# Rotary embedding on half the head: tiles of 64 KB runs, three resident, one product in PSUM, last tile in halves

## The chip, the cores and the metric

One NeuronCore of a Trainium2 chip. Times are device microseconds of the core for one execution; "span" is the time from the first to the last instruction in a profiled execution, about 2 us shorter (160.4 us of 162.49 in the kernel before). Each kernel ran in turns with the kernel before on the same chip. The experiments ran in later jobs, on several chips and not in the changed kernel's rounds, so they are compared with it through the kernel before. An execution over 1.5% above the fastest of the same kernel is classed slow.

## The reference, cut to what matters

```python
x: (16, 512, 16, 64) float32          # batch, seq, heads, dim
x1, x2 = x[..., :32], x[..., 32:]
first  = x1[..., :16] * cos[..., :16] - x1[..., 16:] * sin[..., :16]
second = x1[..., :16] * sin[..., :16] + x1[..., 16:] * cos[..., :16]
out = concatenate([first, second, x2], axis=-1)
```

33.55 MB are read and 33.55 MB written. Half of every row (x2) is only copied. On the other half there are four multiplications and two additions for each pair of elements.

## The kernel before

A tile holds K = 8 sequence positions on each of 128 partitions, a contiguous run of 32 KB a partition, 4 MB in all. There are eight tiles and five buffers. Loads are issued from SP, stores from ACT; both queues draw on the same 16 DMA engines (in the profile before, 49.3% and 48.7% of the time of 16; loads alone, up to 32 us, moved 403 and 437 GB/s, loads and stores together 431 to 433).

```python
K = 8
x_pool = tile_pool(name="xp", bufs=5)
ab_pool = tile_pool(name="abp", bufs=1)
... # cos and sin loaded from ACT, spread to all partitions by 4 VectorE copies
KC = 4
for t in range(T):                                   # T = 8
    x_t = x_pool.tile([P, K, H, D], fp32)
    nc.sync.dma_start(out=x_t..., in_=xf[t])
    for k0 in range(0, K, KC):
        x1 = x_t[:, k0 : k0 + KC, :, 0:HF]
        ...
        nc.vector.tensor_mul(out=a_t[:], in0=x1, in1=c)
        nc.vector.tensor_mul(out=b_t[:], in0=x1, in1=s)
        nc.vector.tensor_sub(out=x1[..., 0:Q],  in0=a_t[..., 0:Q],  in1=b_t[..., Q:HF])
        nc.vector.tensor_add(out=x1[..., Q:HF], in0=a_t[..., Q:HF], in1=b_t[..., 0:Q])
    nc.scalar.dma_start(out=of[t], in_=x_t...)
```

## Time and profile before

| | before |
|---|---|
| time, median | 162.49 us (3 runs) |
| span of the profiled run | 160.4 us |
| both data queues' share of 16 DMA engines | 98.0% |
| VectorE busy | 110.8 us (69%) |
| last tile's data in, last store issued | 128.3 us, 142.1 us |

The lines that carry this stand in the prediction. In the timeline: start, duration, engine, line, operation, output and inputs, count, and in brackets the idle time before it with what ended it.

### The profile page before, as it was taken

To read this page: it belongs to the slowest core of one execution; us is meant where nothing else is said; L and a number is where in the kernel's file an instruction comes from. 1 tells how busy PE (TensorE), PEld (TensorE's weight loads), DVE (VectorE), ACT (ScalarE), POOL (GpSimd) and SP (SyncE) were. 2 spreads that over 40 slices of the span, in tenths; PEclk is the share of its full clock that TensorE was granted. 3 is DMA by queue.
4 is the path that set the end of the run, shared out by engine and by line. 5 is a ranking of instruction groups with operands and counts; after the bars stand their busy time and mean duration, and the time that the engine had idled before them with its cause. 6 is when DMAs were issued, how large, how long until landed. Compare 5 with 4: busy or idle time off the path is not lost.

```text
span 160.4 us, 155 instructions
## 1 busy us (share of the span) xinstructions
DVE 110.8 (69%) x68; POOL 0.2 (0%) x4
## 2 busy tenths in 40 slices
DVE  0001599999999999999998799609995099940000
POOL 0000000000000000000000000000000000000000
DMA  7999999999999999999999999999999999999993
GB/s 253 408 400 408 392 417 490 400 408 498 400 400 474 433 392 457 457 392 449 466 392 417 490 400 408 498 400 400 476 425 400 466 441 400 449 457 400 417 482 147
DMA packets 2465, 67.25 MB, mean 419 GB/s; under 512 B 288, under 2 KB 416, under 8 KB 416
## 3 DMA queue, kind: packets, MB, share of 16 engines
q1 hardware_dynamic: 1152, 33.55, 49.3%
q10 hardware_dynamic: 1312, 33.69, 48.7%
q14 instruction: 1, 0.01, 0.0%
HBM read 33.69 MB, written 33.55 MB: 419 GB/s over the span
## 4 chain that ended last, share of the span: by engine, by line
DMA 53%; DVE 30%; issue 4%; DVEq 1%; ACTq 0%; SPq 0%
DMA x_t<-in_x_dram 21%; DMA out_dram<-x_t 21%; DVE b_t L66 11%; DMA stage<-in_sin_dram 10%; DVE a_t L65 10%; DVE x_t L70 5%; DVE x_t L67 4%; DVEq L99 1%; ACTq L41 0%; DVE table L48 0%; SPq L58 0%; DVEq L65 0%
## 5 line engine op out<-in xcount | busy, mean ns | idle before, releaser
L65 DVE TENSOR_TENSOR a_t<-x_t,table 128x2048 f32<-128x2048 f32 x16 | 36.7, 2292 | 13.6 <-DMA x_t<-in_x_dram 13.2
L66 DVE TENSOR_TENSOR b_t<-x_t,table 128x2048 f32<-128x2048 f32 x16 | 36.5, 2284 | 0.0
L67 DVE TENSOR_TENSOR x_t<-a_t,b_t 128x1024 f32<-128x1024 f32 x16 | 19.6, 1226 | 0.6
L70 DVE TENSOR_TENSOR x_t<-a_t,b_t 128x1024 f32<-128x1024 f32 x16 | 19.5, 1218 | 0.0
L48 DVE COPY table<-stage 64x256 f32<-64x256 f32 x4 | 1.1, 287 | 17.1 <-DMA stage<-in_cos_dram 12.2
L88 POOL MEMSET const-bfloat16-1.0<- 128x1 bf16 x1 | 0.1, 102 | 0.0
L88 POOL MEMSET const-uint8-127<- 128x1 uint8 x1 | 0.1, 102 | 0.0
L88 POOL MEMSET const-float32-0.0<- 128x1 f32 x1 | 0.1, 99 | 0.2 <-issue 0.2
L88 POOL MEMSET const-float32-1.0<- 128x1 f32 x1 | 0.1, 99 | 0.0
## 6 DMA issues: line engine op xcount, KB each, us to landing
x_t<-in_x_dram SPq DMA_DIRECT2D x8, 4096.0 KB, 33.9
out_dram<-x_t ACTq DMA_DIRECT2D x8, 4096.0 KB, 31.3
stage<-in_cos_dram ACTq DMA_DIRECT2D x1, 64.0 KB, 11.4
stage<-in_sin_dram ACTq DMA_DIRECT2D x1, 64.0 KB, 16.3
```

What stands on the lines that cost most here:

```text
L48: nc.vector.tensor_copy(out=table[r * PB : (r + 1) * PB, t], in_=stage[:, t, :, 0:Q].unsqueeze(2).to_broadcast((PB, K, 2, Q)),)
L65: nc.vector.tensor_mul(out=a_t[:], in0=x1, in1=c)
L66: nc.vector.tensor_mul(out=b_t[:], in0=x1, in1=s)
L67: nc.vector.tensor_sub(out=x1[:, :, :, 0:Q], in0=a_t[:, :, :, 0:Q], in1=b_t[:, :, :, Q:HF])
L70: nc.vector.tensor_add(out=x1[:, :, :, Q:HF], in0=a_t[:, :, :, Q:HF], in1=b_t[:, :, :, 0:Q])
L88: nc = _bacc.Bacc("TRN2", target_bir_lowering=False, num_devices=1)
L99: with _tile.TileContext(nc) as tc:
```

## The change

The intent: longer runs per DMA packet and fewer, longer VectorE operations. A tile of K = 16 has runs of 64 KB; three of them are resident. To make room (the author's reckoning), one product goes to PSUM and the other is formed in place. Only the last tile is cut in halves, so that its first half can be computed and stored early. GpSimd takes half of the table copies.

```diff
-    K = 8
+    K = 16
-    x_pool = ctx.enter_context(tc.tile_pool(name="xp", bufs=5))
-    ab_pool = ctx.enter_context(tc.tile_pool(name="abp", bufs=1))
+    x_pool = ctx.enter_context(tc.tile_pool(name="xp", bufs=3))
+    b_pool = ctx.enter_context(tc.tile_pool(name="bp", bufs=1, space=bass.MemoryType.PSUM))
...
+        eng = nc.vector if r % 2 == 0 else nc.gpsimd      # table copies, cos and sin in one
...
-    KC = 4
+    KC = 8
+    loads = [[16]] * (T - 1) + [[8, 8]]
+    stores = [[16]] * (T - 1) + [[8, 8]]
...
-            nc.vector.tensor_mul(out=a_t[:], in0=x1, in1=c)
             nc.vector.tensor_mul(out=b_t[:], in0=x1, in1=s)
+            nc.vector.tensor_mul(out=x1, in0=x1, in1=c)
...              # sub and add now read x1 and b_t; a piece is stored when its last rows are done
```

More of the change, by code (lines that the diff above doesn't have):

```diff
@@ L29 @@
     REP = P // PB
+    R = H * D
     xf = x.rearrange("b s h d -> (b s h d)").rearrange("(t p f) -> t p f", t=T, p=P)
@@ L46 @@
     for r in range(REP):
-        for t in range(2):
-            nc.vector.tensor_copy(
-                out=table[r * PB : (r + 1) * PB, t],
-                in_=stage[:, t, :, 0:Q].unsqueeze(2).to_broadcast((PB, K, 2, Q)),
-            )
+        eng = nc.vector if r % 2 == 0 else nc.gpsimd
+        eng.tensor_copy(
+            out=table[r * PB : (r + 1) * PB].rearrange("p t k c j -> p (t k) c j"),
+            in_=stage.rearrange("p t k j -> p (t k) j")[:, :, 0:Q]
+            .unsqueeze(2)
+            .to_broadcast((PB, 2 * K, 2, Q)),
+        )
     C = table[:, 0].rearrange("p k c j -> p k (c j)")
     Sn = table[:, 1].rearrange("p k c j -> p k (c j)")
-    KC = 4
+    KC = 8
+    loads = [[16]] * (T - 1) + [[8, 8]]
+    stores = [[16]] * (T - 1) + [[8, 8]]
     for t in range(T):
         x_t = x_pool.tile([P, K, H, D], fp32)
-        nc.sync.dma_start(out=x_t.rearrange("p k h d -> p (k h d)"), in_=xf[t])
+        x_f = x_t.rearrange("p k h d -> p (k h d)")
+        k0 = 0
+        for n in loads[t]:
+            nc.sync.dma_start(
+                out=x_f[:, k0 * R : (k0 + n) * R], in_=xf[t, :, k0 * R : (k0 + n) * R]
+            )
+            k0 += n
+        ends, k0 = [], 0
+        for n in stores[t]:
+            ends.append((k0, k0 + n))
+            k0 += n
         for k0 in range(0, K, KC):
@@ L62 @@
             s = Sn[:, k0 : k0 + KC].unsqueeze(2).to_broadcast((P, KC, H, HF))
-            a_t = ab_pool.tile([P, KC, H, HF], fp32)
-            b_t = ab_pool.tile([P, KC, H, HF], fp32)
-            nc.vector.tensor_mul(out=a_t[:], in0=x1, in1=c)
+            b_t = b_pool.tile([P, KC, H, HF], fp32)
             nc.vector.tensor_mul(out=b_t[:], in0=x1, in1=s)
+            nc.vector.tensor_mul(out=x1, in0=x1, in1=c)
             nc.vector.tensor_sub(
-                out=x1[:, :, :, 0:Q], in0=a_t[:, :, :, 0:Q], in1=b_t[:, :, :, Q:HF]
+                out=x1[:, :, :, 0:Q], in0=x1[:, :, :, 0:Q], in1=b_t[:, :, :, Q:HF]
             )
             nc.vector.tensor_add(
-                out=x1[:, :, :, Q:HF], in0=a_t[:, :, :, Q:HF], in1=b_t[:, :, :, 0:Q]
+                out=x1[:, :, :, Q:HF], in0=x1[:, :, :, Q:HF], in1=b_t[:, :, :, 0:Q]
             )
-        nc.scalar.dma_start(out=of[t], in_=x_t.rearrange("p k h d -> p (k h d)"))
+            for lo, hi in ends:
+                if hi == k0 + KC:
+                    nc.scalar.dma_start(
+                        out=of[t, :, lo * R : hi * R], in_=x_f[:, lo * R : hi * R]
+                    )
 _INS = ['x', 'cos', 'sin']
```

## The prediction

> **What bounds the kernel now.** I read the two-line summary of queues first, because the kernel does almost no arithmetic per byte: 33.55 MB in, 33.55 MB out.
>
> ```profile
> DVE 110.8 (69%) x68; POOL 0.2 (0%) x4
> DMA  7999999999999999999999999999999999999993
> ...
> q1 hardware_dynamic: 1152, 33.55, 49.3%
> q10 hardware_dynamic: 1312, 33.69, 48.7%
> ```
>
> The queues' shares are of the time of 16 DMA engines: 49.3 + 48.7 = 98.0%. Only 2.0% of 160.4 us, 3.2 us per DMA engine, is not spent on a packet. VectorE is busy for 69%. The slices show where the 3.2 us lie: 7 in the first slice and 3 in the last, 9 (90% or more) everywhere else. Then the windows, cut where the work changes (columns: stretch, its length, VectorE busy, POOL busy, clock, DMA share, GB/s):
>
> ```profile
> 4.00:20.00 16.00, 2.86 (x5) 0.00 (x0) 1.00 0.98 403
> 20.00:32.00 12.00, 11.90 (x8) 0.00 (x0) 1.00 1.02 437
> 32.00:60.00 28.00, 27.69 (x18) 0.00 (x0) 1.00 1.00 431
> 60.00:100.00 40.00, 37.94 (x22) 0.00 (x0) 1.00 1.00 433
> 100.00:128.00 28.00, 16.72 (x11) 0.00 (x0) 1.00 1.00 431
> ```
>
> Loads alone (to 32 us) and loads with stores (after it) run at the same rate, about 432 GB/s at a share of 1.00: the DMA engines are full, whichever direction. A packet is booked where it ends, so short windows wobble. The rest is the start and the compute times:
>
> ```profile
> 0.73 0.54 ACTq L41 DMA_DIRECT2D stage<-in_cos_dram  x1
> 0.73 93.59 SPq L58 DMA_DIRECT2D x_t<-in_x_dram  x8
> 1.30 0.61 ACTq L42 DMA_DIRECT2D stage<-in_sin_dram  x1
> ...
> 17.67 0.59 DVE L48 COPY table<-stage 64x256 f32<-64x256 f32 x2 [4.90 <-DMA stage<-in_sin_dram]
> 18.29 2.29 DVE L65 TENSOR_TENSOR a_t<-x_t,table 128x2048 f32<-128x2048 f32 x1
> ```
>
> VectorE starts only at 18.29 us because two 64 KB table loads land at 12.2 and 17.7 us, behind the x loads. That lateness is free: the DMA engines are busy with five tiles of loads meanwhile. VectorE later idles three times for a load (13.2 us in the waits), which is also free: it waits for the full DMA engines. The chain of waits puts 53% on DMA and 30% on DVE, but that chain follows the buffers; the DVE part of it (18 to 60 us) lies under full DMA engines.
>
> From the packet records of the trace: a 32 KB packet takes 1213 ns, a 1 KB packet 46 ns, the first data packet starts at 1.7 us and the last completion is at 159.2 us. Each engine has 128 packets of 32 KB: 128 x 1.213 = 155.3 us. With 1.7 us in front and 1.2 us behind that makes 158.2 of the 160.4; some 2 us are gaps and small packets, most before 23 us. The median of 162.49 us is 2.1 us above the span.
>
> [...]the 64 KB cosine load needs 11.4 us to land, its packets taking turns with 32 KB packets of x.[...]
>
> **The change part by part.**
>
> Bytes: the same 67.1 MB. That alone fixes about 155 us.
>
> Runs of 64 KB in place of 32 KB: 46 ns for 1 KB and 1213 ns for 32 KB give (1213 - 46)/31 = 37.6 ns per KB and a fixed part of 46 - 37.6 = 8.4 ns a packet. A 64 KB run should take 2 x 1213 - 8.4 = 2418 ns. Of the 128 packets per engine, the 96 of the first three quarters become 48; the last tile keeps 32 KB. So 48 x 8.4 ns = 0.4 us saved. The DMAs drop from 18 to 12, six completions of 9 ns. So **-0.45 us**, on the path.
>
> VectorE: 64 operations become 32. Half a tile costs [...]2 x 4.42 us and 2 x 2.29 us, 13.4 us, where two quarters of today cost 2 x 6.92 (18.29 to 25.21). Over 8 halves 107 us for 110.7[...]. All beside DMA: **0 us**. What counts is only whether VectorE's times still feed the DMA queues with tiles of 8 MB, four of them, three resident.
>
> Tables: each load is now 32 rows of 2 KB, so 2 packets and a completion per engine in place of 4 and one; but each turn is a 64 KB packet of 2.42 us. Today the first cosine packet starts at 5.9 us, about 3.5 packets of x after 1.7. I take 3 to 3.5 turns of 2.42: 9.5 to 10.2 us. Six turns later (3 for each table) both tables are in at about 22 to 24 us; tile 0, 8 x 2.42 us, lands at about 22 too. Then two copies on VectorE[...] and two on POOL at the side[...]. VectorE starts at about s = 25 to 27 us, not 18.3. Take 26.
>
> The schedule from there, in us, with 19.4 for 8 MB when alone:
> - Loads 0 to 2 (24 MB) keep DMA busy until about 61 (1.7 + 24 x 2.42 + 1.3 of start gaps).
> - Tile 0 is done at 26 + 26.7 = 53 and its store is issued. Today the first store, issued at 32.14, moves data at 36.0, 3.2 packets later; now 3.2 x 2.42 = 7.7, so at about 60: still before the loads run out. Store 0 ends at 61 + 19.4 = 80.5.
> - Tile 1 is done at 53 + 26.7 = 79.4: store 1 is queued just as store 0 ends. The load of tile 3 needs the buffer of tile 0, is issued at 80.5 plus some 0.5 us to signal, and moves data 1 us after that (as today's first load: issued 0.73, moving 1.73). **This is the one thin seam**: store 1 fills it if s is 26, else there is a gap of up to 1.5 to 2 us. I book **+0.5 us**.
> - From 80.5 store 1 and load 3 take turns: both done at about 119.5. Tile 2 is done at 106, so store 2 is queued behind store 1. Half 3a landed at about 100 and is done at 119.5; half 3b lands at 120 and is done at 133.5. Stores 2, 3a, 3b are then 16 MB from 119.5 on: 158.5. Both halves are queued long before their turn, so loading and storing the last tile in halves adds and saves nothing.
>
> Sum: 162.5 - 0.45 + 0.5, less some 0.3 us for fewer small packets at the start (my guess): **162.2 us**.
>
> **The rivals.**
> 1. *The seam opens.* If tables and tile 0 are later (s = 32 or more), store 0 comes after the loads run out at 61 and store 1 some 5 us after store 0 ends. For it: eight-megabyte steps, only three buffers. Against: load 3 fills the second hole after 2 us. It would make 164 to 166.
> 2. *VectorE becomes the bound.* For it: PSUM operands and in-place multiplies are new. Against: it may end its last half as late as about 146 (158 - 9.7 for a 4 MB store, and some margin) against 133.5 expected; 12 us over 107 is 11% slower operations. In that case up to 164.
> 3. *Long runs are better than the line says, or start and tail shrink.* [...]A gain of 2% (3.25 us) would need more than all the time in which DMA is idle now, and the 2.9 us of first and last latency in that are not touched.
> 4. *Long runs are worse* (64 KB cut into pieces[...]). Nothing in the trace speaks for it; 1% of rate is 1.6 us.
>
> **Range and chances.** The byte count fixes 155 us and nothing but gaps can add. [...]likely 161.5 to 162.8, a seam of 2 us 164. Range 161.0 to 164.0. Faster by over 2% needs what rival 3 excludes: 0.02. Slower by over 2% (165.7) needs rival 1 in full or two rivals at once: 0.04. Within 2%: 0.94.
>
> **What the profile after would show.** Queue shares again near 98% in sum, with 1280 data packets of x and not 2048 (if 2048, the runs were cut). VectorE near 108 us busy, 4.42 and 2.29 us operations, first multiply at 25 to 27 us. DMA slices of 9 throughout; a dip only near 60 or 80 us. Last multiply done at about 133. The prediction is wrong if a slice in the middle falls under 9, [...]or if the last store is issued after 146 us.

The sum came to 162.2 us, from 162.5 - 0.45 + 0.5 and less some 0.3. Its 0.3 was a guess at a part of the 2 us of gaps and small packets in the profile before, and is not shown. The profile before alone leads to the same 4.42 us by an estimate: 1226 ns for 1024 elements and 2292 for 2048 are 1066 for 1024 more, so 2292 + 2 x 1066 = 4424 for 4096.

## More of the kernel before

```profile
128.30 2.29 DVE L65 TENSOR_TENSOR a_t<-x_t,table 128x2048 f32<-128x2048 f32 x1 [5.90 <-DMA x_t<-in_x_dram]
...
135.22 2.29 DVE L65 TENSOR_TENSOR a_t<-x_t,table 128x2048 f32<-128x2048 f32 x1
...
140.89 1.22 DVE L70 TENSOR_TENSOR x_t<-a_t,b_t 128x1024 f32<-128x1024 f32 x1
```

The reader is to see that 14 us of VectorE work follow the last load's landing. They cost nothing, because the DMA engines are still full (share 1.04, 447 GB/s, from 128 to 142 us): earlier stores wait in the queue.

## The result, and the profile after

| | before | changed |
|---|---|---|
| median, same rounds | 162.45 us (6 runs) | 171.87 us (6 runs, 170.94 to 174.04) |
| ratio of the fast runs | | 1.056 (95%: 1.0531 to 1.0588) |

A ratio is the mean time of one kernel's fast runs over that of the other's fast runs in the same rounds, so it is not quite the ratio of the medians. The change is 5.6% slower; 162.2 us within 161.0 to 164.0 had been predicted.

The execution profiled with these times was a slow one (173.62 us). The changed kernel was therefore run again unedited, twice. The first of those runs is a single execution with a profile at 174.27 us; its state is unknown, its time that of slow ones. The second, on the chip of a later job, gave 168.23 and 168.54 us as fast and 172.98 and 173.74 as slow executions, with a profile of a fast one (span 166.8 us). Against the mean of the kernel before in that job, 162.5 us, its two fast executions are 3.6% slower (two executions, so without an interval), not 5.6%: how large the loss is differs between jobs. That fast profile, busy tenths in 40 slices and queues' shares:

```profile
DVE 108.9 (65%) x34; POOL 3.2 (2%) x6
DVE  0000439999999999999999999008993001999000
DMA  7979979996997999799698889999888989950885
q1 hardware_dynamic: 720, 33.55, 47.4%
q10 hardware_dynamic: 816, 33.69, 46.7%
```

The shares sum to 94.1%, not 98.0%. Single sevens and sixes in the DMA row are the booking of long packets where they end (around the second 6, from 70 to 95 us, at least 15 packets are in flight in the packet records); the 5 and the 0 late in the row are a real hole. The windows around it (stretch, its length, VectorE busy, POOL busy, clock, DMA share, GB/s):

```profile
108.00:141.00 33.00, 13.34 (x4) 0.00 (x0) 1.00 0.99 429
141.00:149.00 8.00, 7.86 (x2) 0.00 (x0) 1.00 0.91 393
149.00:155.00 6.00, 5.49 (x3) 0.00 (x0) 1.00 0.00 0
155.00:165.00 10.00, 0.00 (x0) 0.00 (x0) 1.00 0.98 419
```

From 149 to 155 us nothing is moved while VectorE computes; then the last 4 MB are stored alone. The timeline says why VectorE is so late:

```profile
81.90 1.03 SPq L68 DMA_DIRECT2D x_t<-in_x_dram  x2
...
113.32 4.43 DVE L81 TENSOR_TENSOR b_t<-x_t,table 128x4096 f32<-128x4096 f32 x1 [9.01 <-DMA x_t<-in_x_dram]
...
126.76 28.13 ACTq L91 DMA_DIRECT2D out_dram<-x_t  x2
141.11 4.43 DVE L81 TENSOR_TENSOR b_t<-x_t,table 128x4096 f32<-128x4096 f32 x1 [14.38 <-DMA x_t<-in_x_dram]
...
152.24 2.28 DVE L86 TENSOR_TENSOR x_t<-x_t,b_t 128x2048 f32<-128x2048 f32 x1
```

The last tile's two loads are issued at 82 us. The first half is used from 113.3 us and the second from 141.1 us. The prediction had 100 and 120. The last store is issued at 154.6 us.

The groups of the VectorE (line, engine, operation, output and inputs, shape, count | busy us, mean ns of one | idle us before, and what ended most of it) show that its operations cost what was predicted:

```profile
L81 DVE TENSOR_TENSOR b_t<-x_t,table 128x4096 f32<-128x4096 f32 x8 | 35.5, 4433 | 26.3 <-DMA x_t<-in_x_dram 26.1
L82 DVE TENSOR_TENSOR x_t<-x_t,table 128x4096 f32<-128x4096 f32 x8 | 35.4, 4425 | 0.3
L83 DVE TENSOR_TENSOR x_t<-x_t,b_t 128x2048 f32<-128x2048 f32 x8 | 18.3, 2288 | 0.3
L86 DVE TENSOR_TENSOR x_t<-x_t,b_t 128x2048 f32<-128x2048 f32 x8 | 18.2, 2280 | 0.0
L50 DVE COPY table<-stage 32x1024 f32<-32x1024 f32 x2 | 2.1, 1056 | 18.8 <-DMA stage<-in_sin_dram 18.8
L50 POOL COPY table<-stage 32x1024 f32<-32x1024 f32 x2 | 2.9, 1474 | 18.4 <-DMA stage<-in_sin_dram 18.4
```

The slow execution with which the median was reported has the same hole, only wider; its slices:

```profile
DVE  0000449999999999999999993008992000999100
DMA  7989995999889996999799989999989999700885
```

There the second half is used from 146.2 us and the last store is issued at 159.6 us. In the packet records the DMA engines are without work for 10.6 us on average before that store, against 6.6 us in the fast profile. The spans exceed that of before by 11.4 and 6.4 us: in these two profiles the hole is the loss, to within 1 us.

### The profile page after: what moved, and what is told of

It reads as the page before. It is cut to its first block, busy times and chain, and to the rows that moved or that the text cites. A ratio compares the mean times of both kernels' runs of the same rounds, so it can differ in the third digit from the quotient of the medians.

```text
span 171.8 us, 108 instructions
## 1 busy us (share of the span) xinstructions
DVE 108.8 (63%) x34; POOL 3.1 (2%) x6
## 4 chain that ended last, share of the span: by engine, by line
DVE 45%; DMA 33%; another core or an unknown queue 9%; issue 3%; DVEq 1%
DMA x_t<-in_x_dram 33%; DVE b_t L81 18%; DVE x_t L82 15%; DVE x_t L86 7%; DVE x_t L83 5%; DVEq L119 1%; DVEq L81 0%
## 5 line engine op out<-in xcount | busy, mean ns | idle before, releaser
L81 DVE TENSOR_TENSOR b_t<-x_t,table 128x4096 f32<-128x4096 f32 x8 | 35.5, 4432 | 31.1 <-DMA x_t<-in_x_dram 30.9
L82 DVE TENSOR_TENSOR x_t<-x_t,table 128x4096 f32<-128x4096 f32 x8 | 35.4, 4424 | 0.3
L83 DVE TENSOR_TENSOR x_t<-x_t,b_t 128x2048 f32<-128x2048 f32 x8 | 18.3, 2286 | 0.3
L86 DVE TENSOR_TENSOR x_t<-x_t,b_t 128x2048 f32<-128x2048 f32 x8 | 18.2, 2280 | 0.0
L50 DVE COPY table<-stage 32x1024 f32<-32x1024 f32 x2 | 2.1, 1056 | 19.1 <-DMA stage<-in_sin_dram 19.1
L50 POOL COPY table<-stage 32x1024 f32<-32x1024 f32 x2 | 2.9, 1474 | 18.8 <-DMA stage<-in_sin_dram 18.7
```

Source lines behind the costliest of these rows:

```text
L50: eng.tensor_copy(out=table[r * PB : (r + 1) * PB].rearrange("p t k c j -> p (t k) c j"), in_=stage.rearrange("p t k j -> p (t k) j")[:, : ...
L82: nc.vector.tensor_mul(out=x1, in0=x1, in1=c)
L83: nc.vector.tensor_sub(out=x1[:, :, :, 0:Q], in0=x1[:, :, :, 0:Q], in1=b_t[:, :, :, Q:HF])
L86: nc.vector.tensor_add(out=x1[:, :, :, Q:HF], in0=x1[:, :, :, Q:HF], in1=b_t[:, :, :, 0:Q])
```

## The experiments

**The theories.** P: the DMA engines take turns between the load queue and the store queue packet by packet. A packet here is a run (in the records of each data queue 384 packets of 64 KB and 256 of 32 KB, in the slow profile), so the last tile's 32 KB load packets beside 64 KB store packets get a third of the rate, not a half. The data comes late, the stores that should cover its computation are used up, and a hole opens. B: with three resident tiles the last load is issued too late, at 82 us, whatever its packets. V: half-tile VectorE operations, 13.4 us before a store can start, are too long at the end, or are slowed by PSUM. "Idle" in what follows is the time for which, by the packet records, fewer than 14 of the 16 DMA engines have a packet, in the middle of the run, as a mean over the engines.

### The last tile loaded whole

```diff
-    loads = [[16]] * (T - 1) + [[8, 8]]
+    loads = [[16]] * T
```

> The last tile is loaded by one DMA in 64 KB runs, everything else as in the changed kernel. Theory P (the DMA engines take turns packet by packet between loads and stores, so a 32 KB load packet beside a 64 KB store packet gets a third of the rate): with equal packets the load gets half, 8 turns of 4.84 us from about 86 us, so the last tile's data is in at about 125 us and not at 146; both its halves are computed by 152, the DMA engines stop for some 3 us instead of 10.6, time about 165 to 166 us. Rival B (three resident tiles: the load is issued too late, at 82 us, whatever its packets): the data is still in at about 146, and now no half of the tile can start before, so the time rises by a half tile's 13.4 us to about 184 us.

Measured: 166.58 us median of 4 (163.65 to 167.3); only the fastest was classed fast, so there is no ratio with an interval. In the profile (a slow one at 166.29 us):

```profile
125.56 4.43 DVE L81 TENSOR_TENSOR b_t<-x_t,table 128x4096 f32<-128x4096 f32 x1 [21.55 <-DMA x_t<-in_x_dram]
...
139.00 4.43 DVE L81 TENSOR_TENSOR b_t<-x_t,table 128x4096 f32<-128x4096 f32 x1
...
150.13 2.28 DVE L86 TENSOR_TENSOR x_t<-x_t,b_t 128x2048 f32<-128x2048 f32 x1
```

With twice the packet, the whole 8 MB are in at 125.6 us, earlier than the second half of it had been, though the load is issued at the same 82.2 us. Idle 3.7 us before the last store, and 0.6 us at 139 us, where the next to last store was issued just as the one before it ended. P had said 125, 152 and some 3 us. The time that it gave, 165 to 166 us, none of the four runs met: the fast one is below it, the slow ones are above. B had said 146, and falls as a sole cause. This is the cleanest of the experiments: only the load differs, one DMA in 64 KB runs in place of two in 32 KB runs.

### Stores in 32 KB runs

```diff
+                    cut = 8 if t < T - 1 else 8
+                    for p0 in range(lo, hi, cut):      # two DMAs in place of one
-                    nc.scalar.dma_start(out=of[t, :, lo*R : hi*R], in_=x_f[:, lo*R : hi*R])
+                        nc.scalar.dma_start(out=of[t, :, p0*R : (p0+cut)*R], in_=x_f[:, p0*R : (p0+cut)*R])
```

> The first three tiles are still loaded in 64 KB runs, computed and stored at the same moments, but each store is two DMAs of half a tile, so that stores move in 32 KB packets like the last tile's two loads. Theory P: the loads get half the rate, first half in at about 103 us, second at about 122, last operation at about 135, no stretch without DMA in the middle, time 161.5 to 163.5 us. Rival B (late issue with three buffers): second half in at about 146 as in the changed kernel, time about 171. Rival V (half-tile VectorE operations are too long at the end): the tail after the last load is the same 13.4 us of operations and a 4 MB store, time about 171.

Measured: 162.04 us median of 4, ratio 0.998 (0.9942 to 1.0017): the loss is gone. The slices show no hole:

```profile
DVE  0000239999999999999999999939990599700000
DMA  7969699699699999999999999999999999999991
```

The first half is used from 107.4 us, the second from 126.8, and the last store is issued at 140.2. P had said 103, 122 and 135: the order is right, the moments are some 4 to 5 us later, for the load moved its first data only at 86.8 us. One thing was not as I had written: the framework let the first of the two stores go as soon as its half was done (the first store of all at 37.4 us, not 50.9), so packets were not all that changed. The last load was issued no earlier for it, at 83.0 us. V falls as a sole cause: the half-tile operations are all still there.

### The mix turned round

```diff
-    loads = [[16]] * (T - 1) + [[8, 8]]
+    loads = [[16]] * T                 # with the 32 KB stores of the experiment above
```

> The mix turned round: last tile loaded whole in 64 KB runs, stores of the first three tiles in 32 KB runs. Theory P: the load gets two thirds of the rate, 8 turns of 3.63 us from about 86 us, so all of the last tile is in at about 115 to 116 us; it is computed at about 142, before the earlier stores have drained, time 161.5 to 163.5 us. Rival B: in at about 146 us, time about 184.

Measured: 162.11 us median of 4, ratio 0.997 (0.9947 to 0.9997).

```profile
81.94 0.33 SPq L68 DMA_DIRECT2D x_t<-in_x_dram  x1
...
114.64 4.43 DVE L81 TENSOR_TENSOR b_t<-x_t,table 128x4096 f32<-128x4096 f32 x1 [10.07 <-DMA x_t<-in_x_dram]
```

Issued at the same moment as in the changed kernel, all 8 MB are in at 114.6 us, where the changed kernel has half of them. P had said 115 to 116.

### The last half in quarters

```diff
-        for k0 in range(0, K, KC):
+        for k0, KC in ((0, 8), (8, 8)) if t < T - 1 else ((0, 8), (8, 4), (12, 4)):
-    stores = [[16]] * (T - 1) + [[8, 8]]
+    stores = [[16]] * (T - 1) + [[8, 4, 4]]
```

> Packets of the loads as in the changed kernel (32 KB loads beside 64 KB stores), but the last half tile is computed and stored as two quarters. Theory P: the second half is still in only at about 146 us; the first quarter is stored from 154 us on while the second is computed until 160, so the last store is 2 MB in place of 4 MB, 4.85 us shorter: about 166.5 us, still over 2% slower than before. If the half-tile operations alone were the cause (rival V), the time would come back to about 162.5.

Measured: 168.62 us median of 4 (167.28 to 169.79), ratio 1.035 (1.0268 to 1.0440). The second half was used from 144.6 us; the hole is cut in two, 3.4 and 2.1 us. The time is some 2 us above what I wrote. Shorter operations at the end don't remove the loss. Whether they soften it is not shown: the ratio is below the 1.056 of the changed kernel's first job, and about the 3.6% of its later one.

### A smaller load packet still

```diff
-    loads = [[16]] * (T - 1) + [[8, 8]]
+    loads = [[16]] * (T - 1) + [[4, 4, 4, 4]]
```

> The last tile's load cut into four DMAs of 16 KB runs; stores stay at 64 KB. Theory P: the load now gets a fifth of the rate as long as stores are queued, so its first half (16 packets of 16 KB per engine, each beside a 64 KB store packet, turns of 3.03 us from about 86 us) is in only at about 134 us and not at 116; the stores then run out and the second half follows alone, in at about 144 to 145 us. Both halves are computed after that, last operation at about 161, time about 174 to 175 us. If the share did not depend on the packet's size, the first half would stay at about 116 us and the time at 171.

Measured: 171.2 us median of 4 (168.46 to 175.16), ratio 1.043 (1.0363 to 1.0498). My numbers missed: the first half was used from 127.7 us (not 134, though not 116 either), the second from 143.0, and the two fast runs took 168.46 and 170.29 us, not 174. The share itself was as P says (table below). What I had left out is that stores with four fifths of the rate (79%, table below) use up their own queue: store 1 was through at about 105 us, the next was issued at 104.8 and moved its first data 3.4 us later, and in between the load had the engines nearly alone (308 GB/s from 104 to 110 us in the packet records). The changed kernel has a smaller patch of the same kind (in its slow profile the load has 99 to 100% of the bytes from 108 to 110 us, at 381 to 389 GB/s), which is most likely why its second half is in at 140.6 us and not at 86 + 16 x 3.63 = 144.

The share of the load in all bytes moved while both queues were full, from the packet records:

| | load / store packets | share by packet sizes | measured, 86 to 104 us |
|---|---|---|---|
| last tile's load in 16 KB | 16 / 64 KB | 20% | 21% |
| changed kernel, fast profile | 32 / 64 KB | 33% | 33% |
| load whole | 64 / 64 KB | 50% | 53% |
| stores in 32 KB | 32 / 32 KB | 50% | 53% |
| mix turned round | 64 / 32 KB | 67% | 73% |

In 18 us there are only 4 to 7 turns, so some points of difference are to be expected.

In all these runs a piece is one DMA, so a smaller packet is also a smaller DMA, and the edits don't tell which of the two sets the share. The packet records do. In the fast profile 155 packets of x start from 86 to 104 us, and 120 of them within 40 ns after the end of other packets, so most likely on the same engine. All 120 belong to the other queue than those that had just ended. If an engine finished a DMA's eight runs before it turned to the other queue, most would belong to the same one. In the other rows 83 to 87% do so where the queue that had just ended is plain; some of their engines end packets together, and then the match can be a wrong one.

### The same mix in the kernel before

```diff
+        n = 8 if t < T - 1 else 4
+        for p0 in range(0, K, n):       # the last tile's load in two DMAs of 16 KB runs
```

> The kernel before, with only its last 4 MB tile loaded in two DMAs of 16 KB runs beside 32 KB stores: the same one-to-two mix of packets as in the changed kernel. Theory P says that this load too gets a third and is in at about 138 us and not at 127.7, but that it costs nothing here: stores for some 12 us more are queued by then, and only 6.9 us of operations follow the landing before the last store is issued, at about 145. Time 162.2 to 163.0 us. If unequal packets slowed the DMA engines as such, the time would rise by a few us.

Measured: 162.52 us median of 4, ratio 1.0006 (0.9990 to 1.0023). The load was delayed as P says, and nothing was lost:

```profile
138.67 2.29 DVE L69 TENSOR_TENSOR a_t<-x_t,table 128x2048 f32<-128x2048 f32 x1 [8.19 <-DMA x_t<-in_x_dram]
...
DMA  6999999999999999999999999999999999999992
```

Between 110 and 126 us the loads had 35% of the bytes, where the kernel before gave them 54%; the packets' sizes say 33 and 50%. The last data is in at 138.7 us, 10 us later than before, yet the last store is issued at 145.6 us and the DMA row has no hole. So unequal packets alone were no loss here, where 6.9 us lie between the last data and the last store; in the changed kernel's fast profile it is 13.5 us, from 141.1 to 154.6, and there they were one.

### VectorE's part alone

The kernel before with PSUM, in place, and one set of operations per 4 MB tile (KC = 8); then the same with KC = 4.

```diff
-    KC = 4                                     # 4 kept in the second kernel
+    KC = 8
-            nc.vector.tensor_mul(out=a_t[:], in0=x1, in1=c)
             nc.vector.tensor_mul(out=b_t[:], in0=x1, in1=s)       # b_t now in PSUM
+            nc.vector.tensor_mul(out=x1, in0=x1, in1=c)
```

> The kernel before with the VectorE part of the change alone: products in PSUM and in place, one set of operations per 4 MB tile instead of two. All theories: VectorE is not the bound, the last load is in at about 128 us, the last operation ends at about 142, time 162.0 to 163.0 us. If PSUM operands or longer operations were a cost, it would show here.

> The VectorE part alone again, unedited, on the same chip as the other half of it: 162.8 to 164.4 us as before if the 0.9% is real, 162.2 to 162.8 if it was that chip.

> The kernel before with products in PSUM and in place, but still two sets of operations per 4 MB tile. The VectorE part alone cost 0.9% in an earlier run. If that came from the PSUM operands or from working in place, it stays at about 163.9 us here; if it came from the longer operations (one set per tile, so the last store is issued 1.3 us later and in one step), this is back at 162.2 to 162.8 us.

Measured: with KC = 8 164.06 us, ratio 1.0088 (1.0047 to 1.0129), and again 163.59, ratio 1.0059 (1.0033 to 1.0085). With KC = 4 162.65 us, ratio 1.0010 (0.9985 to 1.0035). So PSUM and working in place cost nothing that can be seen (in the changed kernel's fast profile the product into PSUM takes 4433 ns, the one in place 4425). The longer operations cost 0.6 to 0.9%, which the first expectation did not have. In both profiles of KC = 8 one DMA engine finishes each load from the fourth on 1.4 to 2.8 us after the other fifteen (in the second the last at 130.2 us, the others by 127.4), and the end shifts with it; with KC = 4 it is at most 0.8 us. Why one engine falls behind was not found. It is not the 5.6%.

### The changed kernel again

> The changed kernel once more, unedited, because its profile so far fell in a slow execution. Expected of a fast one: the same picture, second half of the last tile in at about 144 to 146 us, the DMA engines without work for some 10 us before the last store, span 169 to 170.5 us.

> The changed kernel once more, for a profile of a fast execution: time 171 to 172, second half of the last tile in at about 144 to 146 us, some 10 us without DMA work before the last store.

Measured: as told with the result. For a fast execution I had expected 171 to 172 us, the second half at 144 to 146 us and some 10 us without work; it took 168.5 us, with 141.1 and 6.6 us. I had taken the picture of a slow execution for that of all. What differs most between the three profiles is the spread of the engines. In the fast one the 16 engines end the last load between 140.1 and 140.6 us; in the other two eleven and ten engines end it by 140.9 and the rest only at 144.0 to 146.4. The first half shows the same, by some 3 us. VectorE starts on a load when the last engine is done (in the first slow profile the last of the 16 completions is at 145.76 us, the first use at 146.20), so some 5 to 5.5 us are added to a path that the hole has made critical. What holds those engines back is open. That they do so in the fast runs of the first job too (171 us) is likely by their times, and not shown: none of those was profiled.

## Why the prediction was wrong, point by point

**The step that failed** is in the schedule: "From 80.5 store 1 and load 3 take turns: both done at about 119.5", with "half 3a landed at about 100" and "half 3b lands at 120". I had read from the cosine load (11.4 us to landing) that packets take turns and had measured the durations of packets, and then shared the rate by halves, as if packets were equal. In the kernel before they are (1024 data packets of 32 KB in each queue). In the changed kernel the last tile is the one tile with 32 KB packets, and it is loaded while 64 KB packets are stored: a turn is 1.21 + 2.42 us, and 16 turns are 58 us, not 39. The halves were in at 112.8 and 140.6 us in the fast profile. So the second is some 20 us late: 19 for the longer turns and 5 for the start (data moved from 85.7 us, not 80.5), less some 3.5 for the patch in which the load had the engines nearly alone.

**What followed from it.** The conclusion "loading and storing the last tile in halves adds and saves nothing" fell with it: halves were exactly what made the packets small. All bytes but the last 4 MB are moved by about 149 us at the earliest, since the DMA engines are full nearly until then (share 0.98 and 0.99 from 82 to 108 and 108 to 141 us in the fast profile). So the last store has to be issued by about 148 us, an estimate from the 148.7 us at which the hole of the fast profile begins and the 0.8 us from the issue of its last store to its first data:

| profile | last data used from | last store issued | idle |
|---|---|---|---|
| before | 128.3 | 142.1 | 0 |
| before, last load in 16 KB | 138.7 | 145.6 | 0 |
| stores in 32 KB | 126.8 | 140.2 | 0 |
| mix turned round | 114.6 | 141.5 | 0 |
| load whole, slow | 125.6 | 152.4 | 3.7, and 0.6 earlier |
| changed, fast | 141.1 | 154.6 | 6.6 |
| last tile's load in 16 KB | 143.0 | 156.5 | 5.5, and 2.3 earlier |
| changed, slow | 146.2 | 159.6 | 10.6 |

The profiles whose last store is issued by 145.6 us have no hole; from 152.4 us on there is one, and its sum grows with the lateness. No profile in the table lies between; the quarters at the end, with two last stores of 2 MB, are left out of it. In the kernel before this reserve was 6 us by the same estimate (148 less 142.1), and it stood in no view as such. But the chain of waits had pointed at the place: the prediction puts its VectorE part at 18 to 60 us and passes over a second one, from 128.3 to 142.1 us, which is the last tile.

**Right:** the bound and the byte count; VectorE at 108.9 us busy (about 108 predicted) with 4.42 to 4.43 and 2.28 to 2.29 us operations; 2418 ns for a 64 KB packet (medians of 2418 for stores and 2422 for loads in the records); 1280 data packets of x; its sums, to within 0.3 us. The list of what the profile after would show named "the last store is issued after 146 us" as what would refute it, and that is what happened.

**Wrong without harm:** VectorE began at 24.0 us in the slow profile and not at 26, because the tables were in at 19.1; tile 0, in at 23.9, then set the start. Of the two VectorE copies of the tables the first took 0.68 us and the second, begun while a GpSimd copy ran, 1.43; no run has these copies alone.

**Wrong, a smaller part of the lateness:** I had scaled the delay of a newly issued DMA with the packet, 3.2 packets. It did not scale: a first store issued at 50.9 us moved data at 54.4, 3.5 us later, with 64 KB packets, where before it took 3.9 us with 32 KB; the first table packet moved at 4.9 us, not 9.5 to 10.2. The same delay hit the last load, for which I had counted 1 us: issued at 82, moving at 85.7. That is 2.7 us of the lateness. In these runs the delay was 0.8 to 1.0 us while the engines were idle (the first load and the last store of the fast profile), and 3.4 to 4.8 us from issue to the first data beside a busy queue, the longest in the two runs with 32 KB stores beside 64 KB loads. The prediction's schedule also shares the rate from 80.5 us on, though by its own line before the load moves data only at 82.

**The rivals.** The seam at 80 us stayed closed: in the packet records at least 15 packets are in flight from 70 to 95 us in the fast profile (the 6 in its slices is booking). VectorE as the bound: no. Long runs better or worse as such: neither; the two repaired kernels, with 64 KB loads, run at 162.0 and 162.1 us against 162.4, a difference too small to say anything of it. I gave 4% to a result slower by over 2%, and no rival was about the division of the rate between the two queues.

## What to carry to other kernels

When two DMA queues competed in these runs, each got a share of the bytes about in proportion to its packet size: the last load had 21, 33, 53 and 73% with packets of 16/64, 32/64, equal, and 64/32 KB; work out landings from turns, not from halves. The load that VectorE waited for was late where its packets were shorter than those it competed with (second half used from 141.1 and 143.0 us), and not where they were as long or longer (126.8, 114.6, and loaded whole beside 64 KB stores 125.6). So cutting only the urgent last tile into halves was the wrong way round: cutting the stores too, into 32 KB runs, took the loss away (ratio 0.998). Whether issuing the last load earlier would have done so as well was not tested. Before making the last piece of work longer or later, read how long the DMA queue still has other work once the last load has landed; that reserve, some 6 us in the kernel before, is what hid the piece here.
